# Output projection of a two-layer decoder trunk as seven block products, with its weights prepared during stick attention

## The chip, the cores and the metric

The kernel runs on one core of a Trainium2 chip. The metric is the device time of one execution in microseconds (us), as a median of several runs. PE is TensorE (matmuls), DVE is VectorE, ACT is ScalarE, POOL is GpSimd, SP is the engine whose queue issues nearly all DMAs.

## What is computed

Two layers of a decoder on 1024 tokens with 1024 features, in float32. Each layer adds two mixers and a gated ConvFFN to the residual x:

```
for l in range(2):
    h = rmsnorm(x, norm1[l]);  proj = h @ w_in[l]          # q, k, v of two mixers, and gates
    o_a = dilated_mixture(...)                             # windows of 128, 512 and 2048 tokens, 4 heads each
    o_b = stick_breaking_attention(...)                    # 4 heads, swept in blocks of 128 queries
    g_a, g_b = split(sigmoid(gate_pre + b_gate[l]))
    merged = g_a * (o_a @ w_br[l, :256]) + g_b * (o_b @ w_br[l, 256:])
    x = x + merged @ w_o[l]                                # the output projection
    h2 = rmsnorm(x, norm2[l])
    a, v = split(h2 @ w_up[l])
    x = x + (gelu(causal_conv(a)) * v) @ w_down[l]
return rmsnorm(x, norm_f)
```

## The kernel before

**Numbers in two parts.** PE multiplies fp32r operands, which hold fewer bits than float32. Each operand is therefore two tiles, a rounded high part and the low rest. `split` (L143) makes them: a cast on ACT (L146), a subtraction on DVE (L154). A product is three matmuls, hi x hi, hi x lo and lo x hi.

**Layout.** x lies with features on the 128 partitions: 8 chunks `e` of features, and two halves `n` of 512 tokens (`X[n]`, `xc(n, e)`). It is kept in DRAM (`xs`) during the mixers and fetched by `x_in` in pieces of 1 MB. `H[n]` holds the operand of the next product in two parts.

**Order.** PE's order is the order of the program text (`manual_schedule` over the whole kernel). On the other engines and on SP's queue a scheduler orders the ready instructions by their place in the text; `high_priority` moves one forward, manual dependencies move one back (`yields`, L1044, puts a DVE instruction behind the attention's latest one). Every engine then runs its queue in that order. In the FFN from the end of its second block to its last, ACT, DVE and POOL follow the text too (L1900). Tiles of one tag share a fixed number of buffers: "ot" and "bias" have one, "ql" and "wr" two, "wh", "wl", "xa" and "p4" four, "pt" and "e8" six; each of the four PSUM tags "ps", "s", "t", "o" has two banks.

**A layer.** `mixer` runs the input products of 18 pairs of 128 columns (`pair`, L1159), each as seven block products (Strassen's scheme in Winograd's form: sums of blocks take the place of the eighth product), while `attend` (L375) runs the attention items between their matmuls: 16 stick-breaking items, 4 near items, 16 far items. `Dense.share` (L309) counts the steps: one is half a block product, 6 matmuls, so a pair has 14. `pair_v` (L1289) transposes its values through a PSUM bank "o" (`v_t`) and splits them into a tile `vv` in buffer "ot" (L1295 to L1306); the attention's output `sb_o` uses bank "o" too.

**Branches.** For 16 pairs (n, e) the two branch products are multiplied by their gates (L1476) and added into `mrg` (L1481); `merged` (L1439) makes the two parts for the projection, the high one on ACT, the low one on POOL. `branch_in` (L1429) loads and splits the branch weights of two chunks. `X_AT` names the places where the four pieces of x are asked for.

**Output projection.** `wo_chunk` (L1323) is one of 16 units (n, e), all of half 0 first: load 128 columns of `w_o` (`weights`, L160), split them, 8 k x 3 matmuls, add the result to x on DVE (L1328), and add x squared into the norm's sum (`norm_add`: square on ACT L482, sum on DVE L484). `w_o` is so read and split twice, once for each half.

```
drive(first_half(), relay(*wo, primed=True), 2.5, 36)
```

After 36 steps (9 units) this line starts `first_half` beside the rest: `norm` for half 0 (PE totals L539, root on ACT, a scaling L556, a cast L558 and a subtraction L559 for each chunk) and `first_sum` (L529 and a split, four times). The norm of half 1 is handed to `ffn` and runs there beside the first FFN blocks (`up_plain` 0 and 1, then `up(2)` with seven products; `u_c` is one of its banks). `sums` and the later splits of the FFN run there on ACT and DVE.

**Seven products elsewhere.** `down` already computes the FFN's second half in this way: `into` tells which block of x each product's bank is added to, and one bank serves several products in a row.

Of the kernel before, what the change touches and what calls it, by code (L numbers as in the profile page):

```python
# [49 lines left out]
LEAD_N = 7  # L50
LEAD_T = 3
AHEAD_B = 3
X_AT = (3, 5, 14, 15)
AHEAD = 200
JOIN = 4
SEND = 4
# [4 lines left out]
def f32(ap):  # L61
    return ap.bitcast(F32)
# [3 lines left out]
def trunk_kernel(ctx, tc, x, norm1, w_in, b_gate, w_br, w_o, norm2, w_up, conv_w, conv_b, w_down, norm_f, out, depth=None, probe=None):  # L66
# [51 lines left out]
    xs = [dr.tile([P, KD, HF], F32, name=f"xs{n}") for n in range(2)]  # L118
    gs = dr.tile([KD, 2, P, 2, HF], F32, name="gs")
    gd = dr.tile([NF // 2, 7, P, 2, HF], F32, name="gd")  # L120
    obd = dr.tile([P, 2, T], F32, name="obd")
    tk = [dr.tile([2, 64, 4, 2, 4, 256], F32, name=f"tk{i}") for i in range(2)]
    tv = [dr.tile([2, 4, P, 2, 256], F32, name=f"tv{i}") for i in range(2)]
# [19 lines left out]
    def split(hi, lo, src, turn=None, behind=None):  # L143


        one = act.copy(hi, src)  # L146
        if behind:
            tc.add_manual_dep(one.ins, behind[0], NO_SYNC, reason="behind")
        if turn == "is":
            LAST["act"] = one.ins.name  # L150
        elif turn == "waits" and "act" in LAST:
            tc.add_manual_dep(one.ins, LAST["act"], NO_SYNC, reason="in turn")
        LAST["hi"] = one.ins.name
        two = dve.tensor_tensor(lo, src, f32(hi), ALU.subtract)  # L154
        if behind:
            tc.add_manual_dep(two.ins, behind[1], NO_SYNC, reason="behind")
        if turn == "is":
            LAST["dve"] = two.ins.name
        return two


    def weights(src, cols, place=None, eng=None):

        per = 512 // cols
        got = []
        src = src.rearrange("(k p) n -> p k n", p=P)
        for r in range(0, KD, per):
            raw = sb.tile([P, per, cols], F32, tag="wr", bufs=NRAW, name="w_raw")
            nc.sync.dma_start(raw, src[:, r : r + per, :])
# [12 lines left out]

    def product(o, pairs, first=True, last=True, share=False):

        n = len(pairs)
        quantum = 2 * 512 // o.shape[-1]
        for i, ((lh, ll), (rh, rl)) in enumerate(pairs):
            pe.matmul(o, lh, rh, start=(first and i == 0), stop=False, skip_group_check=share)  # L188
            pe.matmul(o, lh, rl, start=False, stop=False, skip_group_check=share)
            pe.matmul(o, ll, rh, start=False, stop=(last and i == n - 1), skip_group_check=share)  # L190
            if i % quantum == quantum - 1 and i < n - 1:
                yield
# [35 lines left out]
    class Dense:  # L228
# [4 lines left out]
        def __init__(self):  # L233
            self.main, self.plain, self.seven, self.done = [], [], [], set()
            self.side, self.later, self.hooks = [], {}, []
            self.now = self.nxt = None
            self.due, self.count = 0.0, 0
            self.started = False
            self.scored = self.applied = self.kq = self.v = 0
            self.rows, self.near, self.free = 0, 0, [0] * 4  # L240
            self.b = self.n = self.bv = 0

        def choose(self):
            if self.main and self.main[0][1] <= self.done and not (self.plain and self.main[0][3]):
# [64 lines left out]
        def share(self):  # L309
            self.count += 1  # L310
            for f in self.later.pop(self.count, ()):
                f()
            self.fetch()
            return True

# [131 lines left out]
    def h_part(n, k):  # L447
        return H[n][0][:, k, :], H[n][1][:, k, :]
# [9 lines left out]
    def xc(n, e, sub=slice(0, HF)):  # L458
        return X[n][e // 4][:, e % 4, sub]
# [13 lines left out]

    ACC = [None, None]

    def norm_add(n, e, first=False):

        if first:
            ACC[n] = sb.tile([P, HF], F32, tag="ql", bufs=2, name="nrm")
        acc = ACC[n]  # L480
        sq = acc if first else small("sq")
        act.activation(sq, xc(n, e), AF.Square)  # L482
        if not first:
            dve.tensor_tensor(acc, acc, sq, ALU.add)  # L484
# [559 lines left out]
    def yields(one):  # L1044

        for k in ("red", "dve"):
            if k in LAST:
                tc.add_manual_dep(one.ins, LAST[k], NO_SYNC, reason="in turn")
# [271 lines left out]
        return pair(dense, l, (OFF_G + e * P, OFF_G + D + e * P), False, put)  # L1320


    def wo_chunk(l, n, e):  # L1323
        w = weights(w_o[l][:, e * P : (e + 1) * P], P)
        yield
        o = bank("ps", "o_ps")
        yield from product(o, [(w[k], h_part(n, k)) for k in range(KD)])
        dve.tensor_tensor(xc(n, e), xc(n, e), o, ALU.add)  # L1328
        norm_add(n, e, e == 0)
        yield  # L1330

    def mixer(l, pending):
        R.clear()
# [7 lines left out]
            *((None, set(), f, True) for f in (pair_v(dense, l, 2), pair_kq(dense, l, 1, 1), pair_kq(dense, l, 2, 1))),  # L1341
        ]
        dense.side, dense.begin = block_sums(dense, l)
        dense.done |= {"K0", "K1", "V0", "V1", "V2", "V3"} | ({"wv"} if l else set())
        if l:
            next(vectors)
# [38 lines left out]
                items.append((f"T{pr}{i}", [f"F{8 * pr + i}"], [], RATE_T, lambda pr=pr, i=i, share=share: far_item(dense, pr, i // 4, i % 4, share)))  # L1385
        dense.fetch()
        attend(dense, items)
        oh = {}

        def branches():  # L1390
# [38 lines left out]
        def branch_in(i):  # L1429
            if i < len(todo):  # L1430
                e, wb = todo[i][1], big("br_w", F32R)
                raw = sb.tile([P, 4, 256], F32, tag="wr", bufs=NRAW, name="br_raw")
                nc.sync.dma_start(raw, w_br[l].rearrange("(k p) n -> p k n", p=P)[:, :, e * P : (e + 2) * P])
                parts_ = [[wb[:, h, 512 * q : 512 * q + 512].rearrange("p (k n) -> p k n", k=2) for h in range(2)] for q in range(2)]
                for q in (1, 0):
                    split(*parts_[q], raw[:, 2 * q : 2 * q + 2, :])
                wbs.append(parts_)

        def merged(n, e, m):  # L1439
            act.copy(H[n][0][:, e, :], m)  # L1440
            pool.tensor_tensor(H[n][1][:, e, :], m, f32(H[n][0][:, e, :]), ALU.subtract)

        wo = [wo_chunk(l, n, e) for n in range(2) for e in range(KD)]

        for i in range(3):
            gate_load(i)
# [11 lines left out]
        for i, ab in order:  # L1458
            n, e = todo[i]
            sl = slice(n * HF, (n + 1) * HF)  # L1460
            if i not in seen:
                if e == 0:
                    new_h(n)
                if i % 4 == 0:
                    wb = wbs.pop(0)
                if i in X_AT:
                    late_x = X_AT.index(i)
                    x_in(late_x // 2, late_x % 2)
            gt = gts[i]
# [10 lines left out]
            m = small("mrg")  # L1480
# [748 lines left out]
```

## Time and profile before

| | |
|---|---|
| median of 3 runs | 2602.6 us (2602.13 to 2603.34) |
| the profiled execution | 2603.86 us |
| its span, first to last instruction | 2602.2 us |
| granted TensorE clock | 1.000 |
| matmuls | 12647 |
| DMA | 470.60 MB, mean 181 GB/s |

The profile gives for each engine its busy time; for groups of equal instructions the line, the engine, the operation, output and inputs, the count, the sum and the mean duration; for a wait the instruction that ended it. Matmuls overlap: one of 389 ns starts 227 ns after another. A page's number behind "x" is a count.

### The profile page before, as it was taken

How to read it: one execution, taken by the hardware profiler on the slowest of the kernel's cores; microseconds unless marked ns; L12 is line 12 of the kernel's file. 1: busy time of each engine (PE TensorE's matmuls, PEld its weight loads, DVE VectorE, ACT ScalarE, POOL GpSimd, SP SyncE). 2: the span in 40 equal slices, each digit the busy share in tenths (PEclk: the TensorE clock that was granted, in tenths of full speed). 3: DMA queues.
4: the chain of work that ended last, by engine and by line, in shares of the span. 5: the costliest groups of instructions: out<-in, count | busy, mean ns of one | idle time of the engine just before them, and what ended most of it. 6: DMA issues, size and time to landing. Idle time of an engine off the chain costs nothing.

```text
span 2602.2 us, 36060 instructions
## 1 busy us (share of the span) xinstructions
PE 2589.6 (100%) x12647; PEld 2165.4 (83%) x12647; DVE 2084.7 (80%) x3485; ACT 1349.5 (52%) x2521; POOL 105.6 (4%) x145
## 2 busy tenths in 40 slices
PE   9999999999999999999999999999999999999999
PEld 8888888888888888888888888888888888888887
DVE  8877777796888888897677788777869888889965
ACT  6555666664554545422445555666645555554225
POOL 3000000030000000000000000000300000000000
PEclk9999999999999999999999999999999999999999
DMA  7434578863244454688344436798633354447863
GB/s 257 152 119 134 163 207 226 236 235 101 88 148 157 138 176 134 243 325 311 146 147 146 128 127 194 194 235 238 198 99 121 122 171 136 154 162 264 342 242 118
DMA packets 401409, 470.60 MB, mean 181 GB/s; under 512 B 24500, under 2 KB 315980, under 8 KB 399436
## 3 DMA queue, kind: packets, MB, share of 16 engines
q1 hardware_dynamic: 400364, 465.90, 55.2%
q0 software_dynamic: 704, 2.13, 0.4%
q8 instruction: 100, 1.64, 0.3%
q14 instruction: 81, 0.66, 0.1%
q10 hardware_dynamic: 160, 0.27, 0.0%
HBM read 305.59 MB, written 162.63 MB: 180 GB/s over the span
## 4 chain that ended last, share of the span: by engine, by line
PE 93%; DVE 3%; ACT 2%; DMA 1%; issue 1%; SPq 0%; POOL 0%; DVEq 0%; ACTq 0%
PE u_a L1060 6%; PE u_a L1061 6%; PE u_a L1059 6%; PE d_ps L1823 5%; PE d_ps L1825 5%; PE d_ps L1824 5%; PE i_a L1059 5%; PE i_a L1060 5%; PE i_a L1061 5%; PE u_c L1059 3%; PE u_c L1060 3%; PE u_c L1061 3%; PE i_c L1059 2%; PE i_c L1061 2%; PE i_c L1060 2%; PE o_ps L188 2%
## 5 line engine op out<-in xcount | busy, mean ns | idle before, releaser
L146 ACT CAST w_hi<-up_a 128x512 fp32r<-128x512 f32 x280 | 174.0, 622 | 277.1 <-DVE up_a L1677 120.8
L154 DVE TENSOR_TENSOR w_lo<-up_a,w_hi 128x512 fp32r<-128x512 f32 x280 | 189.3, 688 | 83.6 <-ACT w_hi L146 83.6
L146 ACT CAST w_hi<-in_a 128x512 fp32r<-128x512 f32 x252 | 156.2, 622 | 161.8 <-PE i_c L1060 35.6
L154 DVE TENSOR_TENSOR w_lo<-in_a,w_hi 128x512 fp32r<-128x512 f32 x252 | 172.7, 687 | 73.3 <-ACT w_hi L146 64.7
L1834 DVE TENSOR_TENSOR x<-x,d_ps 128x512 f32<-128x512 f32 x220 | 149.9, 683 | 60.3 <-PE d_ps L1825 57.0
L1059 PE MATMUL u_a<-hh,w_hi 128*128 128x512 f32 x320 | 124.5, 389 | 0.0
L1060 PE MATMUL u_a<-hl,w_hi 128*128 128x512 f32 x320 | 124.5, 389 | 0.0
L1061 PE MATMUL u_a<-hh,w_lo 128*128 128x512 f32 x320 | 124.5, 389 | 0.0
L1059 PE MATMUL u_a<-t_hi,w_hi 128*128 128x512 f32 x320 | 124.5, 389 | 0.0
L1060 PE MATMUL u_a<-t_lo,w_hi 128*128 128x512 f32 x320 | 124.5, 389 | 0.0
L1061 PE MATMUL u_a<-t_hi,w_lo 128*128 128x512 f32 x320 | 124.5, 389 | 0.0
L1823 PE MATMUL d_ps<-gd_in,w_hi 128*128 128x512 f32 x316 | 123.2, 390 | 0.0
L1825 PE MATMUL d_ps<-gd_in,w_lo 128*128 128x512 f32 x316 | 123.0, 389 | 0.0
L1824 PE MATMUL d_ps<-gd_in,w_hi 128*128 128x512 f32 x316 | 122.9, 389 | 0.0
L1059 PE MATMUL i_a<-hh,w_hi 128*128 128x512 f32 x288 | 117.9, 410 | 0.0
L1059 PE MATMUL i_a<-t_hi,w_hi 128*128 128x512 f32 x288 | 116.5, 404 | 0.0
L1061 PE MATMUL i_a<-hh,w_lo 128*128 128x512 f32 x288 | 113.1, 393 | 0.0
L1061 PE MATMUL i_a<-t_hi,w_lo 128*128 128x512 f32 x288 | 113.1, 393 | 0.0
L1060 PE MATMUL i_a<-hl,w_hi 128*128 128x512 f32 x288 | 112.9, 392 | 0.0
L1060 PE MATMUL i_a<-t_lo,w_hi 128*128 128x512 f32 x288 | 112.9, 392 | 0.0
L1823 PE MATMUL d_ps<-gd_in,wd 128*128 128x512 f32 x284 | 111.0, 391 | 0.0
L1825 PE MATMUL d_ps<-gd_in,wd 128*128 128x512 f32 x284 | 110.5, 389 | 0.0
(405 smaller groups left out, 7738.7 us busy)
## 6 DMA issues: line engine op xcount, KB each, us to landing
gd<-g SPq DMA_DIRECT2D x154, 512.0 KB, 3.1
gd_in<-gd SPq DMA_DIRECT2D x154, 512.0 KB, 6.2
up_a<-in_w_up_dram SPq DMA_DIRECT2D x80, 512.0 KB, 5.5
in_a<-in_w_in_dram SPq DMA_DIRECT2D x72, 512.0 KB, 5.4
wd_raw<-in_w_down_dram SPq DMA_DIRECT2D x22, 1024.0 KB, 11.4
gin<-gs SPq DMA_DIRECT2D x32, 512.0 KB, 4.3
w_raw<-in_w_o_dram SPq DMA_DIRECT2D x64, 256.0 KB, 2.8
gs<-u SPq DMA_DIRECT2D x48, 256.0 KB, 2.5
```

The source lines that it names most:

```text
L146: one = act.copy(hi, src)
L154: two = dve.tensor_tensor(lo, src, f32(hi), ALU.subtract)
L188: pe.matmul(o, lh, rh, start=(first and i == 0), stop=False, skip_group_check=share)
L1059: pe.matmul(o, w[0][:, c], rh, start=(first and i == 0), stop=False, skip_group_check=True)
L1060: pe.matmul(o, w[0][:, c], rl, start=False, stop=False, skip_group_check=True)
L1061: pe.matmul(o, w[1][:, c], rh, start=False, stop=(last and i == 3), skip_group_check=True)
L1823: pe.matmul(o, wh[:, c], gh, start=(i == 0 and k in (0, 4, 5)), stop=False, skip_group_check=True)
L1824: pe.matmul(o, wh[:, c], gl, start=False, stop=False, skip_group_check=True)
L1825: pe.matmul(o, wl[:, c], gh, start=False, stop=(i == m - 1), skip_group_check=True)
L1834: dve.tensor_tensor(x, x, o, ALU.add)
```

## The change

The output projection becomes seven block products in `out_proj`, with four blocks of 128 rows to a product. Features of the merged branches are divided into even and odd chunks, tokens into the two halves, output features into two halves of 512. The sums of weight blocks that this scheme needs and their two parts don't depend on data: `prepare` makes them for each layer during stick attention, a step of it per counted step from the 15th on, and keeps them in DRAM (`wod`, 7 x 4 tiles of 512 KB). The parts of the branch weights are made and kept in the same way (`brd`); `branch_in` only loads them. The sums of the merged branches are made on DVE beside the branches (`merged`) and beside the first products (`beside`). The sums of squares of both halves lie in buffer "ot". `first_half` starts after 42 of 56 steps of `out_proj`, with its first four steps spread by hand.

```
-X_AT = (3, 5, 14, 15)
+PREP = 14
...
+    wod = dr.tile([7, 4, P, 2, 512], F32, name="wod")
+    brd = dr.tile([4, P, 2, T], F32, name="brd")
...
         def share(self):
...
+            if self.prep and self.count > PREP:
+                next(self.prep, None)
...
-    def wo_chunk(l, n, e):
-        w = weights(w_o[l][:, e * P : (e + 1) * P], P)
...
+    def prepare(l):
+        many = 0
+        def out(src, there):
+            nonlocal many
+            t = small("w_two", F32R) if many % 2 else sb.tile([P, 512], F32R, tag="bias", name="w_two")
+            many += 1
+            act.copy(t[:, 0:256], src)
+            yields(dve.tensor_tensor(t[:, 256:512], src, f32(t[:, 0:256]), ALU.subtract))
+            nc.sync.dma_start(there, f32(t).rearrange("p (h n) -> p h n", h=2))
...
+        for e2 in range(4):
+            blocks = load(w_br[l].rearrange("(k p) n -> p k n", p=P)[:, :, 256 * e2 : 256 * e2 + 256])
+            for _ in range(3):
+                yield
+            for k, x in enumerate(blocks):
+                out(x, brd[e2][:, :, 256 * k : 256 * k + 256])
+                yield
+        for i in range(4):
+            for c in range(2):
+                raw = sb.tile([P, 2, 2, 256], F32, tag="ot", name="w_one")
...
+                for k, x in ((0, a11), (3, a22), (4, a12)):
+                    out(x, wod[k, i][:, :, col])
+                    yield
+                for k, dst, x, y, op in (
+                    (2, a11, a11, a21, ALU.subtract),
+                    (5, a21, a21, a22, ALU.add),
+                    (1, a22, a22, a11, ALU.subtract),
+                    (6, a12, a12, a22, ALU.subtract),
+                ):
+                    into(dst, x, y, op)
+                    out(dst, wod[k, i][:, :, col])
+                    yield
+    def out_proj(keep):
+        order = (0, 4, 1, 2, 3, 5, 6)
+        into = ((0, 0), (1, 0), (1, 1), (0, 1), (0, 0), (1, 1), (1, 0))
...
+        acc = sb.tile([P, 2, HF], F32, tag="ot", name="nrm")
+        def load(at):
...
+                if at % 2 == 0:
+                    if i % 2 == 0:
+                        t = sb.tile([P, 2, 2, 512], F32R, tag="ql", bufs=2, name="wo_in")
+                    nc.sync.dma_start(f32(t[:, i % 2]), wod[k, i])
...
+                else:
+                    w = [sb.tile([P, 512], F32R, tag=tag, bufs=4, name="wo_in") for tag in ("wh", "wl")]
+                    for h in range(2):
+                        nc.sync.dma_start(f32(w[h]), wod[k, i][:, h, :])
...
+        def beside(k, e):
+            c11, c12, c21 = keep[0, 0], keep[1, 0], keep[0, 1]
+            if k == 0:
+                dve.tensor_tensor(c11[:, e, :], c12[:, e, :], c11[:, e, :], ALU.add)
...
+                split(*sums[1][e], c11[:, e, :])
+            elif k == 4:
+                dve.tensor_tensor(c21[:, e, :], c21[:, e, :], c11[:, e, :], ALU.subtract)
...
+                split(*sums[2][e], c12[:, e, :])
+                if e == 3:
+                    x_in(1, 0)
+            elif k == 1:
...
+                split(*sums[3][e], c21[:, e, :])
+                if e == 3:
+                    x_in(1, 1)
+                    x_in(0, 1)
+        load(0)
+        load(1)
         yield
...
+        for at, k in enumerate(order):
...
+            for e in range(4):
+                o, c = banks[k][e], slice(e * P, (e + 1) * P)
+                for i in range(4):
+                    (wh, wl), (gh, gl) = ws[k][i], part(k, i)
+                    pe.matmul(o, wh[:, c], gh, start=(i == 0 and k in (0, 4, 5)), stop=False, skip_group_check=True)
+                    pe.matmul(o, wh[:, c], gl, start=False, stop=False, skip_group_check=True)
+                    pe.matmul(o, wl[:, c], gh, start=False, stop=(i == 3), skip_group_check=True)
+                    if i == 1:
+                        yield
+                n, f = into[k]
+                x = xc(n, 4 * f + e)
+                with tc.high_priority(offset=AHEAD):
+                    dve.tensor_tensor(x, x, o, ALU.add)
+                beside(k, e)
+                if k > 2:
+                    norm_add(n, 4 * f + e, e == 0 and k in (4, 5), acc[:, n, :])
+                yield
+            load(at + 2)
...
         def branch_in(i):
...
-                raw = sb.tile([P, 4, 256], F32, tag="wr", bufs=NRAW, name="br_raw")
-                nc.sync.dma_start(raw, w_br[l].rearrange("(k p) n -> p k n", p=P)[:, :, e * P : (e + 2) * P])
+                nc.sync.dma_start(f32(wb), brd[e // 2])
...
-                for q in (1, 0):
-                    split(*parts_[q], raw[:, 2 * q : 2 * q + 2, :])
...
         def merged(n, e, m):
...
+            hi, lo = H[n][0][:, e, :], H[n][1][:, e, :]
+            if n and e % 2 == 0:
+                t = small("mrg")
+                dve.tensor_tensor(t, m, keep[0, 0][:, e // 2, :], ALU.subtract)
+                split(hi, lo, t)
+                return
+            act.copy(hi, m)
+            pool.tensor_tensor(lo, m, f32(hi), ALU.subtract)
+            if n:
+                other = keep[1, 0][:, e // 2, :]
+                dve.tensor_tensor(other, m, other, ALU.subtract)
...
-                if i in X_AT:
-                    late_x = X_AT.index(i)
-                    x_in(late_x // 2, late_x % 2)
+                if i == 6:
+                    x_in(0, 0)
...
-            if i == 12:
-                next(wo[0])
+            if i == 9:
+                wo = out_proj(keep)
+                next(wo)
...
-        drive(first_half(), relay(*wo, primed=True), 2.5, 36)
+        side = first_half()
+        for n in (42, 0, 0, 2, 1):
+            for _ in range(n):
+                next(wo)
+            next(side)
+        drive(side, wo, 1.0)
```

More of the change, by code (lines that the diff above doesn't have):

```diff
@@ L241, in __init__ @@
             self.b = self.n = self.bv = 0
+            self.prep = None
         def choose(self):
@@ L474, in trunk_kernel, with norm_add @@
     ACC = [None, None]
-    def norm_add(n, e, first=False):
+    def norm_add(n, e, first=False, room=None):
         if first:
-            ACC[n] = sb.tile([P, HF], F32, tag="ql", bufs=2, name="nrm")
+            ACC[n] = room if room is not None else sb.tile([P, HF], F32, tag="ql", bufs=2, name="nrm")
         acc = ACC[n]
@@ L1320, in pair_gate, with into, load @@
         return pair(dense, l, (OFF_G + e * P, OFF_G + D + e * P), False, put)
-    def wo_chunk(l, n, e):
-        w = weights(w_o[l][:, e * P : (e + 1) * P], P)
-        yield
[L1326 to L1330, printed above, removed]
+    def prepare(l):
[7 more added lines that the diff above has]
+            nc.sync.dma_start(there, f32(t).rearrange("p (h n) -> p h n", h=2))
+        def into(dst, a, b, op):
+            yields(dve.tensor_tensor(dst, a, b, op))
+        def load(src):
+            raw = sb.tile([P, 4, 256], F32, tag="ot", name="w_one")
+            nc.sync.dma_start(raw, src)
+            return [raw[:, i, :] for i in range(4)]
+        for e2 in range(4):
[8 more added lines that the diff above has]
+                raw = sb.tile([P, 2, 2, 256], F32, tag="ot", name="w_one")
+                for j in range(2):
+                    src = w_o[l][(2 * i + j) * P : (2 * i + j + 1) * P, :].rearrange("p (f n) -> p f n", f=2)
+                    nc.sync.dma_start(raw[:, j], src[:, :, 256 * c : 256 * c + 256])
+                a11, a21, a12, a22 = (raw[:, j, f, :] for j in range(2) for f in range(2))
+                for _ in range(3):
+                    yield
+                col = slice(256 * c, 256 * c + 256)
+                for k, x in ((0, a11), (3, a22), (4, a12)):
[10 more added lines that the diff above has]
+                    yield
@@ L1343, in mixer @@
         dense.side, dense.begin = block_sums(dense, l)
+        dense.prep = prepare(l)
         dense.done |= {"K0", "K1", "V0", "V1", "V2", "V3"} | ({"wv"} if l else set())
@@ L1387, in mixer @@
         attend(dense, items)
+        for _ in dense.prep:
+            pass
         oh = {}
@@ L1431, in branch_in, with merge @@
                 e, wb = todo[i][1], big("br_w", F32R)
-                raw = sb.tile([P, 4, 256], F32, tag="wr", bufs=NRAW, name="br_raw")
-                nc.sync.dma_start(raw, w_br[l].rearrange("(k p) n -> p k n", p=P)[:, :, e * P : (e + 2) * P])
+                nc.sync.dma_start(f32(wb), brd[e // 2])
                 parts_ = [[wb[:, h, 512 * q : 512 * q + 512].rearrange("p (k n) -> p k n", k=2) for h in range(2)] for q in range(2)]
-                for q in (1, 0):
-                    split(*parts_[q], raw[:, 2 * q : 2 * q + 2, :])
                 wbs.append(parts_)
-        def merged(n, e, m):
-            act.copy(H[n][0][:, e, :], m)
-            pool.tensor_tensor(H[n][1][:, e, :], m, f32(H[n][0][:, e, :]), ALU.subtract)
-        wo = [wo_chunk(l, n, e) for n in range(2) for e in range(KD)]
+        keep = {}
+        def merge(n, e):
+            if e < 2 and (n, e) != (1, 1):
+                keep[n, e] = quarter("m_part")
+            return small("mrg") if n and e % 2 else keep[n, e % 2][:, e // 2, :]
+        def merged(n, e, m):
+            hi, lo = H[n][0][:, e, :], H[n][1][:, e, :]
[3 more added lines that the diff above has]
+                split(hi, lo, t)
+                return
+            act.copy(hi, m)
[3 more added lines that the diff above has]
+                dve.tensor_tensor(other, m, other, ALU.subtract)
         for i in range(3):
@@ L1479, in mixer @@
                 continue
-            m = small("mrg")
+            m = merge(n, e)
             dve.tensor_tensor(m, gt[:, 0, :], gt[:, 1, :], ALU.add)
```

25 lines of the change are left out of this document (added).

## The prediction

> **What bounds the kernel now.** I read the page from the top: busy shares first, then the chain that ended last.
>
> ```profile
> PE 2589.6 (100%) x12647; PEld 2165.4 (83%) x12647; DVE 2084.7 (80%) x3485; ACT 1349.5 (52%) x2521; POOL 105.6 (4%) x145
> PE 93%; DVE 3%; ACT 2%; DMA 1%; issue 1%; SPq 0%; POOL 0%; DVEq 0%; ACTq 0%
> ```
>
> TensorE (PE) is busy over the whole span and holds 93% of the chain; DVE is second, with a fifth of the span idle. So a removed matmul is worth its full pitch, and an added DVE instruction is free only where DVE idles. Next I read the chain in time order inside the output projection, for the pitch, and a table by window, for where DVE idles. The columns of the table are window, length, then the busy time of PE, PEld, DVE, ACT and POOL, the clock, the DMA share and GB/s.
>
> ```profile
> 625.84 0.23 PE o_ps L190
> ...
> 628.56 0.23 PE o_ps L190
> 90.00:280.00 190.00, 189.73 (x968) 157.54 (x967) 148.60 (x235) 103.87 (x212) 12.44 (x24) 1.00 0.42 130
> 530.00:581.00 51.00, 51.00 (x231) 42.19 (x229) 48.27 (x64) 31.78 (x54) 19.47 (x14) 1.00 0.73 250
> 590.00:668.00 78.00, 78.00 (x352) 64.59 (x350) 50.49 (x79) 33.23 (x56) 0.00 (x0) 1.00 0.34 100
> 637.00:668.00 31.00, 31.00 (x138) 25.53 (x137) 26.59 (x42) 15.89 (x27) 0.00 (x0) 1.00 0.32 94
> 668.00:719.00 51.00, 51.00 (x231) 41.95 (x230) 48.40 (x86) 28.66 (x50) 0.00 (x0) 1.00 0.29 93
> 1954.00:2005.00 51.00, 50.78 (x229) 41.74 (x228) 48.36 (x85) 28.28 (x50) 0.00 (x0) 1.00 0.29 93
> ```
>
> From the first row of the chain to the last lie 12 matmuls: 2.72/12 = 0.227 us each. The windows are, for layer 0, most of stick attention (90 to 280), the branches (530 to 581), the output projection (590 to 668), its end, and the FFN's first 51 us (668 to 719; layer 1's are 1954 to 2005). DVE idles 41.4 us of the 190, 27.5 of the 78, but only 2.6 of the 51. That last stretch ends in the one place where the chain leaves PE for long in layer 1:
>
> ```profile
> 1999.16 0.60 DVE up_a L1683
> 1999.76 0.60 DVE g L154
> 2000.36 0.61 DVE up_a L1684
> ...
> 2004.52 0.49 ACT u L1696
> ...
> 2005.05 0.50 PE u_c L1059
> PE u_c L1059 <- ACT u L1696: 0.3, 1, 0.3
> ```
>
> DVE, then ACT behind it, release the matmul `u_c` of the third FFN block. The wait is 0.3 us: at this point DVE's queue is exactly as late as PE can bear. I take its slack there as zero.
>
> **Removed: matmuls.** Per layer the old projection issues 2 halves x 8 chunks x 8 k x 3 = 384 matmuls of 128x512, the new one 7 products x 4 chunks x 4 blocks x 3 = 336. That is 48 less, in two layers 96 x 0.227 = **21.8 us**. The loops fix the count; that it isn't saved is no rival. If nothing else moved, the time would be 2602.6 - 21.8 = 2580.8.
>
> **Added in stick attention.** `prepare` issues per layer 16 + 8x7 = 72 casts on ACT, 72 + 32 = 104 DVE instructions, and on SP 72 writes of 256 KB and 20 loads (6.3 MB). All are 256 wide; the nearest rows, and how DVE instructions of 512 follow each other:
>
> ```profile
> L751 DVE TENSOR_TENSOR beta<-beta,stay 128x512 f32<-128x512 f32 x32 | 21.5, 682 | 1.6
> L751 DVE TENSOR_TENSOR beta<-beta,stay 128x255 f32<-128x255 f32 x16 | 6.7, 419 | 1.0 <-DVE stay L744 0.5
> L724 ACT ACTIVATE beta<-z 128x256 f32<-128x256 f32 x16 | 6.2, 390 | 4.9 <-PE z L650 4.9
> 703.12 0.68 DVE L1659 TENSOR_TENSOR b_f<-b_f,b_f 128x512 f32<-128x512 f32 x1
> 703.72 0.68 DVE L154 TENSOR_TENSOR t_lo<-b_f,t_hi 128x512 fp32r<-128x512 f32 x1
> 704.33 0.68 DVE L1662 TENSOR_TENSOR b_f<-b_f,b_f 128x512 f32<-128x512 f32 x1
> 159.38 0.68 DVE L154 TENSOR_TENSOR sbl<-sb_t,sbh 128x512 fp32r<-128x512 f32 x1
> 163.14 0.40 PE L665 MATMUL sb_o<-sbl,kv 128*66 128x256 f32 x2
> gs<-u SPq DMA_DIRECT2D x48, 256.0 KB, 2.5
> L169 SPq DMA_DIRECT2D w_raw<-in_w_o_dram x5: 367/368/368, 639.7 to 650.6; - x5
> ```
>
> An instruction of 0.68 us lets the next start after 0.60, so 0.08 us overlap; 256 wide I put at 0.42 - 0.08 = 0.34, and 104 x 0.34 = 35 us. The 108 steps, at 14 steps per weight pair, fill about these 190 us. DVE would be busy 184 of 190 us: covered on average, but with no spare. The second cover is lead: `sbl` is written 3.1 us before its matmul (159.38 + 0.68 against 163.14). ACT gains 72 x 0.39 = 28 us on 103.9: no bound. DMA gains 18.9 + 6.3 MB in 190 us, 133 GB/s beside 130: share 0.42 to about 0.85. SP spends 92 x 0.37 = 34 us on the issues; behind them in its queue stand the loads of keys, values and weight pairs, which are asked for some steps ahead. A cast into a `w_two` buffer waits until that buffer's last write has landed (2.5 us for 256 KB), and the sigmoids and `sbh` casts stand behind it on ACT; every second one takes the single buffer "bias". Bounds per layer: below nothing is excluded, as these 104 instructions replace none in this window; above, 43 - 41 = 2 us of overflow plus about 3 us if each bad stretch also uses up the lead. I take 1.5, nearer the low end, because the added instructions are ordered behind the attention's.
>
> [...]
>
> **Moved into the branches.** The eight splits of branch weights leave (each a cast and a subtraction), and about five of projection weights; 12 DVE instructions come: for the second half's even chunks a subtraction and a low part that POOL did, and for its odd ones another difference. 12 against 13: nothing changes on 48.27 busy of 51. SP's queue there now loads 1 MB per branch weight (was 0.5), 4 MB of projection weights and 1 MB of x (was 4): about 17 MB in 51 us where 250 GB/s makes 12.8. Cover is the three chunks' lead. Cost 0 to 2, I take 0.
>
> **DMA of the projection.** Each product needs 2 MB of ready parts, loaded while the product between runs: 48 x 0.227 = 10.9 us.
>
> ```profile
> gd_in<-gd SPq DMA_DIRECT2D x154, 512.0 KB, 6.2
> x<-xs SPq DMA_DIRECT2D x8, 1024.0 KB, 6.1
> 540.00:550.00 10.00, 10.00 (x45) 8.29 (x45) 8.90 (x11) 4.67 (x9) 4.29 (x4) 1.00 0.90 340
> ```
>
> At 340 GB/s 2 MB last 6.2 us; with 1 MB of x ahead in the queue 9.3, plus issue and landing about 1.5. That just fits 10.9. If x comes late, its add holds the accumulating bank, and PE behind it. 0 to 4 per layer, I take 0.5.
>
> **The end of the projection, the main cost.** Before, half 0 of x was final after 8 of 16 chunks, 43.5 us before the end. Now its last block (the fifth product) leaves two products, 21.8 us; the norm's first scaling may start after 44 of 56 steps, 12 x 6 x 0.227 = 16.3 us before the end. The norm, `first_sum` and the x adds of the last two products then crowd DVE ahead of a stretch that has no room. Count from 637.0, where the old norm starts, to 719:
>
> ```profile
> L556 DVE SCALAR_TENSOR_TENSOR b_f<-x,g,nrm_b x8: 737/741/748, 637.0 to 653.1; 128x512 f32<-128x512 f32 x8
> L529 DVE TENSOR_TENSOR s<-b_f,b_f x4: 681/681/684, 661.4 to 669.2; 128x512 f32<-128x512 f32 x4
> L1328 DVE TENSOR_TENSOR x<-x,o_ps x6: 677/686/689, 638.4 to 665.6; 128x512 f32<-128x512 f32 x6
> L484 DVE TENSOR_TENSOR nrm<-nrm,sq x6: 681/682/693, 640.2 to 667.4; 128x512 f32<-128x512 f32 x6
> L154 DVE TENSOR_TENSOR w_lo<-w_raw,w_hi x11: 682/685/693, 639.0 to 666.2; 128x512 fp32r<-128x512 f32 x11
> ```
>
> DVE was busy 26.59 + 48.40 = 75.0 us. Out go the old projection's 6 adds, 6 sums of squares and 7 of the 11 low parts (4 are the FFN's): 19 x 0.60 = 11.4. In come 7 adds and 7 sums of squares after the norm may start: 8.4. That is 72.0 us of work in 16.3 + 51 = 67.3: **4.7 us too much per layer**, and before it DVE can do none of it, since x isn't final and the FFN weights' buffers are held by the sixth product. From below: `first_sum` (8 instructions, 4.8 us) isn't needed until the third FFN block's fifth product, so all could slide: 0. From above, with 3 us of gaps: 8. I take 5. It doesn't matter whether PE stands still at the FFN's first weights or at `u_c`: the queue is the same.
>
> **Sum.** 21.8 - 2 x (1.5 + 0 + 0.5 + 5) = 7.8 us. The profiled execution took 2603.86 (span 2602.2 and 1.7 around it), 1.3 over the median of 2602.6; the gain is a difference and applies to either: 2602.6 - 7.8 = **2594.8**. About 0.2% (5.2 us) is what a measurement of this kernel can tell from no change.
>
> **Rivals.** *Nothing stalls.* `first_sum` slides behind, the lead covers stick attention; only 1 us goes per layer: 2602.6 - 21.8 + 2 = 2583. For it: in the branches DVE is busy 48.27 of 51 us and PE all 51. Against: the 0.3 us wait at `u_c`.
>
> *The gain is eaten.* The end costs 8 and stick attention 2.5 per layer: 2602.6 - 21.8 + 21 = 2602. For it: the 2.6 idle of 51.
>
> *Slower: one buffer held.* The raw weights of `prepare` sit in the only buffer of tag "ot" for 7 to 10 steps, about 18 us, one after the other; `pair_v` needs the same buffer for `vv` four times in this window.
>
> ```profile
> 240.00 0.60 PE L1295 MATMUL v_t<-ident,u 128*128 128x128 f32 x4
> 240.35 0.42 PE L663 MATMUL sb_o<-sbh,kv 128*128 128x256 f32 x2
> 241.20 0.59 ACT L1300 CAST vv<-v_t 128x512 fp32r<-128x512 f32 x1 [1.24 <-DMA sv<-vv]
> ```
>
> ACT's copy already waits 1.24 us for that buffer. A later `vv` keeps `v_t` in one of two banks "o", which `sb_o` needs 0.35 us behind on in-order PE; each `vv` then waits for the one before to be stored (3 us) and converted (1.3). Once the raw weights hold the buffer past the second `v_t`, PE stops for 4.5 to 9 us per layer. At 7.5 with the rest of the sum: 2594.8 + 15 = 2610. Against: ready instructions may run ahead of their step.
>
> **How the numbers follow.** The forecast (faster by 5.2 to 15) 0.42, nothing stalls 0.17, eaten (within 5.2) 0.19, slower 0.22. Faster 0.59, same 0.19, slower 0.22. The range 2582 to 2613 leaves out a little on either side; the forecast's own is 2588 to 2597.4.
>
> **What would show it.** Right: 96 matmuls fewer; 76 us per layer for the seven products (336 x 0.227); DVE full from the rescaling of half 0 to the third FFN block, with PE waiting there some 5 us per layer, on FFN weights or `u_c`; PE waits in stick attention under 2 us per layer. Wrong: a PE wait on bank "o" or `vv` near the first `v_t`; waits on `wo_in` or x; or no waits at the end.

## The result, and the profile after

The changed kernel takes 2699.26 us (2697.25 to 2703.17, four runs) for 2602.97 of the kernel before (2602.13 to 2603.68): slower, with a ratio of 1.0372 (1.0354 to 1.0390). The forecast was 2594.8, and the range ended at 2613. The profiled execution took 2700.12 us, its span 2698.4; the mean granted clock was 0.984, where it had been 1.000.

The rows of the page that answer to those of before, matmuls and engines, then the granted clock in 40 slices:

```profile
PE 2602.4 (96%) x12551; PEld 2164.6 (80%) x12551; DVE 2150.6 (80%) x3701; ACT 1361.9 (50%) x2609; POOL 111.4 (4%) x137
...
PEclk9998999999999999999999989999999999999999
```

The 96 matmuls are gone: 12551 for 12647. Yet PE now idles 4% of the span, and it was busy longer than before, 2602.4 us for 2589.6: some matmuls ran slower. The list of PE's waits names who ended them (columns: us in total, times, the longest):

```profile
PE u_ps L192 <- DVE w_lo L156: 15.1, 2, 7.5
PE v_t L1300 <- DVE vv L1306: 13.2, 2, 6.7
PE v_t L1300 <- DVE ob L678: 9.7, 2, 5.1
PE br_ps L190 <- DMA br_w<-brd: 9.0, 3, 4.3
PE sb_o L668 <- DVE ob L678: 8.5, 2, 4.5
PE i_c L1064 <- ACT u L1217: 7.2, 4, 2.2
PE z L654 <- ACT stay L730: 6.7, 6, 2.7
PE sb_o L668 <- DVE vv L1306: 6.7, 2, 3.3
```

To place the loss I matched PE's matmuls of the two traces in order and followed how late each starts (the delay ledger). In layer 0 the delay grows to 43.6 us in stick attention (90 to 330 us), stays flat until the branches, grows there by 6.4, shrinks by 11.8 in the projection, and grows by 9.9 at the FFN's first matmuls: 48.1. Layer 1 repeats it: 41.8 + 7.5 - 10.9 + 9.8 = 48.2. Together 96.3, as measured. The table by window shows the same (columns as in the prediction; the fourth stretch is 78 us of the seven products):

```profile
90.00:280.00 190.00, 166.82 (x797) 135.07 (x797) 149.14 (x274) 98.68 (x223) 9.31 (x19) 0.94 0.66 211
240.00:260.00 20.00, 14.63 (x63) 11.73 (x63) 14.64 (x28) 7.25 (x17) 0.86 (x2) 0.83 0.58 178
260.00:280.00 20.00, 10.21 (x46) 8.05 (x45) 9.67 (x19) 6.88 (x14) 0.00 (x0) 0.74 0.43 152
...
626.00:704.00 78.00, 78.00 (x352) 64.63 (x350) 47.91 (x75) 21.95 (x38) 2.05 (x2) 1.00 0.47 176
```

Seven products run without a gap. In stick attention PE does 797 matmuls where it did 968, and in the worst 20 us no engine is full: PE 10.21, DVE 9.67, ACT 6.88, DMA 0.43. Nothing there lacks throughput; engines wait for each other. The timeline of ACT just before shows how (start, length, instruction, and in brackets the idle time before it and what ended it):

```profile
243.72 0.58 ACT L148 CAST sbh<-sb_t 128x512 fp32r<-128x512 f32 x1
...
247.78 0.41 ACT L1337 CAST w_two<-w_one 128x256 fp32r<-128x256 f32 x1 [2.71 <-DMA wod<-w_two]
248.09 0.62 ACT L148 CAST w_hi<-in_a 128x512 fp32r<-128x512 f32 x1
252.82 0.40 ACT L1337 CAST w_two<-w_one 128x256 fp32r<-128x256 f32 x1 [4.11 <-DMA w_one<-in_w_o_dram]
253.13 0.47 ACT L148 CAST sbh<-sb_t 128x384 fp32r<-128x384 f32 x1
253.63 0.37 ACT L677 COPY fold<-sb_o 64x256 f32<-64x256 f32 x1
...
267.55 0.59 ACT L1305 CAST vv<-v_t 128x512 fp32r<-128x512 f32 x1 [0.49 <-DVE w_two L1338]
271.92 0.59 ACT L1305 CAST vv<-v_t 128x512 fp32r<-128x512 f32 x1 [3.79 <-DMA sv<-vv]
```

A cast of `prepare` stands at the head of ACT's queue until a transfer lands: first the last write out of its buffer (2.71 us), then the load that it reads (4.11 us). The attention's `sbh` and `fold` come right behind the second cast, 0.3 and 0.8 us later. `fold` could have run since 248.1, when the matmuls of its `sb_o` ended (247.67 in PE's rows below); it ran at 253.63, DVE's `ob` behind it at 254.11, and only this freed the bank for PE's `v_t` at 254.57. The load was late itself: SP's queue held two writes before it, and "ot" the tile before it, and both waited for the low part that DVE made at 248.22 from the cast of 247.78:

```profile
245.79 3.40 SPq L1339 DMA_DIRECT2D wod<-w_two  x2
249.24 1.28 SPq L1361 DMA_DIRECT2D w_one<-in_w_o_dram  x2
```

The first `vv` waits for the buffer "ot" until the last raw weights in it are converted, 24 us after the first `v_t` (243.89) and 13 after the second, and the second `vv` until the first is stored. PE's side of it:

```profile
243.89 0.60 PE L1300 MATMUL v_t<-ident,u 128*128 128x128 f32 x4
...
247.67 0.40 PE L670 MATMUL sb_o<-sbl,kv 128*66 128x256 f32 x2
...
254.57 1.12 PE L1300 MATMUL v_t<-ident,u 128*128 128x128 f32 x4 [5.14 <-DVE ob L678]
...
268.92 1.11 PE L1300 MATMUL v_t<-ident,u 128*128 128x128 f32 x4 [6.44 <-DVE vv L1306]
...
273.38 0.66 PE L668 MATMUL sb_o<-sbh,kv 128*128 128x256 f32 x2 [3.35 <-DVE vv L1306]
```

### The profile page after: what moved, and what is told of

It reads as the page before. It is cut to its first block, busy times and chain, and to the rows that moved or that the text cites. A ratio compares the mean times of both kernels' runs of the same rounds, so it can differ in the third digit from the quotient of the medians.

```text
span 2698.4 us, 36486 instructions
## 1 busy us (share of the span) xinstructions
PE 2602.4 (96%) x12551; PEld 2164.6 (80%) x12551; DVE 2150.6 (80%) x3701; ACT 1361.9 (50%) x2609; POOL 111.4 (4%) x137
## 5 line engine op out<-in xcount | busy, mean ns | idle before, releaser
L1337 ACT CAST w_two<-w_one 128x256 fp32r<-128x256 f32 x144 | 57.5, 410 | 111.0 <-DVE w_one L1342 43.8
L1973 PE MATMUL d_ps<-gd_in,wd 128*128 128x512 f32 x284 | 111.0, 391 | 0.0
```

Of the source, the lines that this page charges most:

```text
L1337: act.copy(t[:, 0:256], src)
L1973: pe.matmul(o, wh[:, c], gh, start=(i == 0 and k in (0, 4, 5)), stop=False, skip_group_check=True)
```

## The experiments

The theory, "held queue": in stick attention `prepare` puts instructions that wait for transfers, buffers or other engines at the head of in-order queues, and holds the single buffer "ot" when `vv` needs it. Rivals: too many instructions for DVE; too much traffic; engines and transfers that slow each other down. The two smaller losses, at the branches and at the end, are tested apart.

**Which part of `prepare`: all left out, engines alone, transfers alone, a pause.** The first three let the projection load constants, as the expectations say.

```
# e1:  dense.prep = nothing;  wo_in and br_w load constants (woz, brz)
# e2:  out() without its write, sources = ones.to_broadcast([P, 256])
# e3:  loads and writes alone, the writes straight from w_one
# e4:  if self.prep and self.count > PREP and not 92 < self.count < 109:
```

> prepare is left out (the projection and the branches load constants of the same size from DRAM, written once). The ledger of the two traces puts some 43 us per layer on stick attention, 6 on the branches, 9 on the end of the projection, and 11 gained by it. If all that stick attention lost comes from prepare: 2699 - 86 = 2613 (2605 to 2620), with PE waits in the window from 90 to 330 us back under 1 us per layer and the waits at the branches and at the FFN's first weights still there. If the loss lies in the new projection's own order or buffers: above 2680.

> prepare keeps its 72 casts and 104 DVE instructions of 256 columns per layer at the same steps, but they read a constant: no loads, no writes, no buffer 'ot'. Theory 'held queue' (casts at the head of ACT's in-order queue wait for transfers, and the raw weights hold the buffer that vv needs): within 6 us of the kernel without prepare, so about 2613 to 2620. Rival 'too many instructions for DVE': most of the 86 us stay, 2670 to 2700.

> prepare keeps its 20 loads into 'ot' and its 72 writes of 256 KB per layer, written straight from the loaded tile, but no cast and no DVE instruction (so the writes carry unsplit data and the projection loads constants). Rival 'traffic' (25 MB more in these windows slow everything): 2680 to 2700. 'Held queue': nothing on ACT or DVE waits for a transfer but vv for its buffer, so between the kernel without prepare (2613) and 2640, with PE waits on v_t alone.

> prepare makes no step in the 16 counted steps from 93 to 108, in which pair_v of the first group turns its values through buffer 'ot'; all else is as in the changed kernel. If the shared buffer 'ot' (the rival of the prediction, one buffer held) is the main cause, the four waits on v_t and sb_o go, 38 us in both layers by the list of waits, and the half-speed stretches behind them: 2640 to 2660. If the casts that wait for landings are the main cause: 2690 or more.

Measured: 2619.16, 2627.87, 2629.32 and 2679.52 us (before: 2602.93). Without `prepare` 80 us go. Of the 2619 some 5 us are, as an estimate, the writing of the constants, which delays the start by a wait of 3.3 us that the changed kernel hasn't got, and slow matmuls after it (2.2 us beyond a wait of 7.55 in the last section); so 2614, as the ledger had it. The wait, and the window of stick attention, as full as before the change:

```profile
PE x_t L2213 <- ACT w_hi L2200: 3.3, 1, 3.3
```

```profile
90.00:280.00 190.00, 189.73 (x966) 157.37 (x966) 148.24 (x234) 104.11 (x211) 11.43 (x24) 1.00 0.42 133
```

All engine work without transfers costs 9 us in both layers (at most 6 were expected), all transfers without engine work 10; together they cost 80. So neither DVE's count nor the traffic is the cause. Nor do the two slow each other down: a cast of `prepare` took 405 ns (median) without transfers and 406 with them, a low part 412 and 419, and a write into `wod` landed after 2.9 us without the engines' work and 2.5 with it. The cost comes of one waiting for the other. In e3 the raw weights hold "ot" for the same counted steps, and yet PE doesn't wait on `v_t` at all, where such waits had been expected: without casts that come late, the shared buffer alone doesn't stop PE there. The pause gains 20 where 40 to 60 were expected: "ot" is a part, not the whole.

**Loads or writes.**

```
# e7:  -  nc.sync.dma_start(there, ...)           (out() without its write)
# e8:  -  raw = sb.tile(..., tag="ot", name="w_one"); its loads   (sources = ones)
```

> prepare with its loads, casts and DVE instructions, but without its 72 writes per layer (the projection and the branches load constants instead). Casts then wait for loads, never for a w_two buffer to be stored. Engines alone cost 9 and transfers alone 10 us over the kernel without prepare (2619). If the landings of loads are what holds the queues: 2655 to 2690. If those of the writes are: 2630 to 2640.

> prepare with its casts, DVE instructions and 72 writes per layer, but without its 20 loads and without buffer 'ot' (the sources are constants, the projection and the branches load constants). If the landings of writes hold the queues: 2655 to 2690. If those of the loads and the buffer 'ot' do: 2630 to 2640. If either alone is harmless and only the two in a row are not, both kernels stay under 2640.

Measured: 2685.12 and 2655.90. Each alone does harm, as if both branches of the expectation were true: with loads 66 us over no `prepare`, with writes 37 (all three kernels write the constants). In the run without loads ACT waits for buffers to be stored, in layer 0 from 90 to 340 us:

```profile
ACT w_two L1339 <- DMA wod<-w_two: 27.2, 19, 5.1
ACT w_two L1339 <- DMA brd<-w_two: 14.0, 7, 3.7
```

and PE waits 2.6 us on `v_t` in all, for 13.2 + 9.7 in the changed kernel. The loads are the larger part and bring the `v_t` waits with them.

**More lead, and "ot" kept clear.** e9 gives a load five steps instead of three before its first cast. e10 does so too, and starts no load that would still hold "ot" in the steps in which `pair_v` turns its values.

```
# e9 and e10:
-            for _ in range(3):            # both places
+            for _ in range(5):
-PREP = 14                                 # 6 in e9, 2 in e10
# e10:
+            while not all(not a - 12 < dense.count < b for a, b in ((93, 107), (135, 149))):
+                yield
+            t = small("w_two", F32R) if many % 2 or dense.count > 134 else ...
```

> The changed kernel with five steps instead of three between a load of raw weights and the first cast of it (and prepare begins 8 steps earlier, so that it ends as before). Loads of 3 to 6 us then have about 9 instead of 5 us. If ACT and DVE are held by the landing of loads: 2650 to 2680. If buffer 'ot', now held longer by each raw tile when vv needs it, is the larger part: 2699 or more.

> As the last, but no raw tile is loaded that would still be held in the steps in which pair_v turns its values, so 'ot' is free for vv (prepare begins at step 3, and after step 134 its parts go to the buffers 'pt' alone). If loads and 'ot' together are the cause, only the waits for the landings of writes stay, worth 28 us by the kernel without loads: 2640 to 2660. If the loss comes with the amount of work and traffic: 2680 or more.

Measured: 2708.58 and 2675.27. Lead alone makes it 9 us slower, but e9 is no clean test. Its twelve tiles take 24 steps more in all, and it begins only 8 earlier; so `prepare` ends 16 steps later, not as before (its last low part is made at 351.0 us instead of 329.6 in layer 0). Where `pair_v` first turns its values, layer 0 loses 17 us instead of 25.5. But now `prepare` holds "ot" when `pair_v` turns the next ones, where the changed kernel has no wait on `v_t`, and PE waits there for 5.7 us. PE's waits on `v_t` in e9, over both places and layers:

```profile
PE v_t L1300 <- DVE vv L1306: 21.6, 7, 6.1
```

In e10 no wait on `v_t` is left, and the time falls by 33 from e9 and by 24 from the changed kernel; 2675 is more than the 2640 to 2660 expected. `prepare` now runs on beside the near windows, and waits stand there instead (PE's waits in e10, its window from 280 to 420, and that of the kernel without `prepare`):

```profile
PE o L670 <- DVE p0l L156: 8.0, 6, 1.6
...
PE i_b L1064 <- DVE u L1228: 6.1, 5, 2.5
```

```profile
280.00:420.00 140.00, 129.35 (x669) 106.87 (x668) 111.52 (x236) 86.38 (x204) 5.28 (x8) 0.96 0.77 227
```

```profile
280.00:420.00 140.00, 140.00 (x772) 119.37 (x771) 110.35 (x232) 87.25 (x204) 4.06 (x6) 1.00 0.68 191
```

**Which queue holds the rest.** From e10: DVE's sums two steps ahead of their casts (e13); casts on GpSimd (e14); no writes (e15). From e12 (below): all of `prepare`'s transfers in GpSimd's queue (e17); each write a step later, with a third `w_two` buffer (e18).

```
# e13: into(*sums.pop(0)) in the steps of k = 3, 4, 2, 5 instead of 2, 5, 1, 6
# e14: -  act.copy(t[:, 0:256], src)    +  pool.tensor_copy(t[:, 0:256], src)
# e17: nc.sync.dma_start -> nc.gpsimd.dma_start in prepare
# e18: if held: nc.sync.dma_start(*held.pop());  held.append((there, t));  many % 3
```

> The kernel of 2675 (raw tiles clear of vv, five steps of lead) with each DVE sum of weight blocks issued two steps before the cast that reads it. If casts that wait for sums hold ACT and with it the attention (8 to 20 us of ACT waits per layer in the changed kernel): 2645 to 2665. If those waits are harmless, as the kernel without transfers (2628) suggests: within 4 of 2675.

> The kernel of 2675 with the 72 casts per layer on GpSimd, whose queue holds little else here than the masks of beta. If ACT's queue, held at the head by casts, is what stops the attention: 2630 to 2650. If DVE's queue (its subtractions wait for the same casts) does as much, or GpSimd slows DVE: 2670 or more.

> The kernel of 2675 without the 72 writes per layer (projection and branches load constants; this costs about 5 us at its start). If the remaining loss is the waits for landings of writes: 2630 to 2645. If it is the loads and the sums: 2660 or more.

> The kernel of 2659 (raw tiles clear of vv, lead 5, branch weights earlier, end reordered) with prepare's loads and writes issued from GpSimd's queue instead of SP's. If what is left of the writes' cost is SP's held queue: 2630 to 2645. If it is the buffers that wait for their landing, or GpSimd's queue now holds the masks of beta in the same way: 2655 or more.

> The kernel of 2659 with each write of prepare issued at its next part, one step (about 1.7 us) later, when the low part is mostly there, and with a third w_two buffer in rotation ('bias' every third time instead of every second). If SP's queue, held 32 us per layer by writes that wait for DVE, costs time: 2640 to 2650. If the landings that the buffers wait for cost as much as before, or nothing of it matters: within 4 of 2659. Not below 2638, since engines and transfers of prepare alone cost 9 and 10 us over 2619 and the end keeps some 3 us per layer.

Measured: 2673.86, 2691.63, 2651.92, 2710.37 and 2656.14 (2651.17 to 2657.48). With the sums ahead ACT no longer waits for them (0.2 us for 11.1, from 90 to 400 us), but it waits longer for writes into `wod` (13.2 for 5.6), and the time stays (e13). The writes still cost 23 us, or some 28 without the 5 us that the constants cost e15; its time lies between the two that were expected. Moving work to GpSimd, which is almost idle (4% of the span in the changed kernel), made things worse, by 16 over e10 (e14) and by 51 over e12 (e17), as the second branch of each expectation had it. The waits of GpSimd in e17, 90 to 360 us, point to why: its queue now stands for DVE's low parts. Behind them in that queue are the attention's masks of `beta`, which its output needs:

```profile
POOL wod L1343 <- DVE w_two L1342: 52.1, 21, 6.8
POOL brd L1343 <- DVE w_two L1342: 15.0, 7, 4.4
```

By these waits it is the same mechanism on another queue; no run separates it from the longer instructions there (for e14 a cast of 683 ns instead of 406, see the last section). e18 gains 3 us on e12's 2659; its interval doesn't separate that from nothing, so whether SP's held head costs anything stays open.

**The branches.** `br_w` is asked for one chunk earlier.

```
                 if i % 4 == 0:
                     wb = wbs.pop(0)
+                    branch_in(i + 4)
...
-            if i % 4 == 1:
-                branch_in(i + 3)
```

> The changed kernel, with the branch weights of the next four chunks asked for one chunk earlier in the text (as the first of four begins instead of after the second), ahead of two loads of gates in SP's queue. If the wait on br_w comes from its place in SP's in-order queue, behind gate loads that wait for DVE: 4.3 us and about 2 of half-speed matmuls per layer go, 2684 to 2692. If the transfers there are limited by bandwidth (17 MB in 51 us): within 4 us of 2699.

Measured: 2696.34, a gain of 3 where 7 to 15 were expected. The number falls on the expectation's other branch, bandwidth, but its reason doesn't hold: the wait on `br_w` is gone, and the delay ledger falls by 6.6 us there; 3 of them come back at the projection's first products, whose operand POOL now delivers too late:

```profile
PE o_ps L1448 <- POOL hl L1585: 1.7, 2, 1.4
```

**The end.** First the FFN's low parts ahead in the queue (e5), then `first_sum` out of the way as well (e11), then all three edits with e10 (e12).

```
# e5:  with tc.high_priority(offset=AHEAD): split(hi, lo, raw)      (first FFN block)
# e11: e5, and
-            yield from first_sum()
+            up_plain(0, ..., {0: first_sum(), 2: both})
```

> The changed kernel, with the casts and low parts of the first FFN block's weights moved ahead of the norm in ACT's and DVE's queues (high priority). If the wait at the FFN's first matmuls is a matter of order (the low parts stand behind the whole norm and first_sum, though their casts are done 20 us earlier), the two waits of 7.5 us and the half-speed matmuls behind them go: 2680 to 2686. If DVE simply has too much work there, as the prediction had it, the wait moves to the norm's own parts or to u_c and the time stays above 2692.

> The changed kernel with the first FFN block's low parts ahead (as in the earlier run in which the wait moved to the norm of half 1) and with first_sum, 8 DVE instructions and 4.8 us per layer, moved from between the projection and the FFN into the first FFN block. If DVE has about 5 us too much before the norm of half 1: that wait falls from 7.5 to about 3 us per layer and the time to 2685 to 2692. If it isn't the amount: within 3 of 2699 or above.

> The three edits together: raw tiles clear of vv with five steps of lead, branch weights asked for one chunk earlier, low parts ahead and first_sum in the FFN. If the three losses add up as the ledger has them: the second kernel of this call, less 3 for the branches, less 8 to 14 for the end, 2625 to 2645; nowhere below the kernel before (2602), since engines and transfers of prepare alone cost 9 and 10 us over 2619. If the edits only move waits: within 5 of the second kernel.

Measured: 2707.28, 2696.06 and 2659.29. In e5 the wait doesn't go; it moves to the norm of half 1, at full size:

```profile
PE nrm_t L545 <- DVE nrm L490: 14.7, 3, 7.5
```

With eight instructions (4.8 us per layer) moved out of the way as well, it shrinks to this (e11):

```profile
PE nrm_t L545 <- DVE nrm L490: 6.0, 3, 2.9
```

So DVE has too much to do there, and order alone doesn't help. The time falls only to 2696, 4 above the 2685 to 2692 expected: per layer 4.6 us of wait go and some come back as new ones. All edits together (e12) reach 2659, 16 better than e10, within the expected sum (3 + 8 to 14), though alone the same edits had given 3 (e6) and 3 (e11); 40 better than the change, 57 worse than before; the expected 2625 to 2645 had e10 too low.

**A last set of edits together.**

> Raw tiles clear of vv, lead 5, sums two steps ahead, casts on GpSimd, branch weights one chunk earlier, low parts ahead and first_sum in the FFN. If all losses add up and the edits take them away: 2605 to 2630. If GpSimd's queue or its share of DVE's time takes ACT's place: 2650 to 2670.

Measured: 2663.56, 4 us over e12; by e13 and e14 the casts on GpSimd are what costs, but no run shows it beside the other edits. No version here beats the kernel before. What costs e12 its last 40 us over the kernel without `prepare` (more, if the losses at the branches and at the end, which that kernel still has, are counted out) isn't settled beyond this: the writes are 23 to 28 of e10's excess, and the rest is spread over short waits.

## Why the prediction was wrong

**What failed.** The step "Added in stick attention": 1.5 us per layer, bounds up to 5. Measured: 43 in the delay ledger, and 40 per layer by leaving `prepare` out (42.6 without the 5 us at that kernel's start). I compared busy sums with idle time (DVE 35 us of work in 41 idle) and called the work covered. That comparison held for the work itself: casts and DVE instructions alone cost 4.4 us per layer, close to the upper bound. It said nothing of instructions that wait. I had named the mechanism, "a cast into a `w_two` buffer waits until that buffer's last write has landed, and the sigmoids and `sbh` casts stand behind it on ACT", and gave it no term of its own. The reason for the low end, that added instructions are ordered behind the attention's, is what the trace refutes: `sbh` at 253.13 came behind a cast that had waited 4.11 us.

**The rival "one buffer held"** had the right place and mechanism, `vv`, `v_t` and bank "o". Its price was 4.5 to 9 us per layer; the steps of the ledger at `v_t` and the `sb_o` behind it add up to 22 in layer 0, 25.5 with the slow matmuls after them. About half of the 22 is not the buffer alone: `v_t` at 254.57 and `sb_o` at 304.19 waited for `ob`, the first of them because `fold` was held on ACT. Keeping "ot" clear gave back 24 in both layers, since other waits took the place. "Ready instructions may run ahead of their step" spoke against it; in the trace they didn't.

**Branches**: predicted 0, measured 7 per layer, 4.3 of it one wait for `br_w`. "Cover is the three chunks' lead" failed because SP's queue is in order: the load was issued only after four gate loads had stood for DVE (columns as in the timeline above):

```profile
599.05 8.05 SPq L1548 DMA_DIRECT2D gin<-gs  x4
607.19 0.38 SPq L1565 DMA_DIRECT2D br_w<-brd  x1
```

**DMA of the projection**: 0.5 predicted; no wait on `wo_in` or x. Right, or slightly too much.

**The end**: 5 predicted, 9.9 measured, of which 7.7 is the step at the wait and 2.2 slow matmuls behind it. The sum of DVE's work, 72.0 us in 67.3, pointed at the place, and that order doesn't matter (e5) was right too. Too small was the assumption that DVE works without a gap before: it idled 2.36 us for PE in the middle.

```profile
687.06 0.69 DVE L1455 TENSOR_TENSOR x<-x,o_ps 128x512 f32<-128x512 f32 x1 [2.36 <-PE o_ps L1449]
```

**Matmuls**: 96 fewer, 11.8 and 10.9 us less in the ledger, 10.9 worked out.

**Missing from the sum**: what a wait costs beyond itself, in the last section.

## What to carry to other kernels

Before hiding work beside a busy stage, compare its waits, not its busy time: for each added instruction ask what it waits for, how long that takes to land, and whose instruction is next in the same in-order queue. Work that costs 9 us without its transfers and 10 without its engines cost 80 with both. By e17, a queue that is idle isn't free when something critical sits in it, and more lead undoes itself where it holds a single shared buffer into the steps that need it (e9).

## What the runs showed of the hardware

After some of its longer waits PE's matmuls run at half speed for a while. After the 7.55 us wait for the FFN's low parts:

```profile
711.81 0.80 PE L192 MATMUL u_ps<-hh,w_lo 128*128 128x512 f32 x1 [7.55 <-DVE w_lo L156]
712.40 0.63 PE L190 MATMUL u_ps<-hh,w_hi 128*128 128x512 f32 x1
...
715.81 0.63 PE L192 MATMUL u_ps<-hh,w_lo 128*128 128x512 f32 x1
...
717.58 0.39 PE L191 MATMUL u_ps<-hl,w_hi 128*128 128x512 f32 x1
717.81 0.39 PE L192 MATMUL u_ps<-hh,w_lo 128*128 128x512 f32 x1
```

From 712.40 to 715.81 eight steps take 3.41 us, 0.426 each; from 717.58 the next starts after 0.23. By the delay against the kernel before, this costs 2.2 us beyond the wait. A wait of 2.66 us was enough, and the slow stretch then began 1.4 us after PE had started again and lasted about 3.5:

```profile
217.07 0.50 PE L654 MATMUL z<-kv,slots 128*128 128x512 f32 x1 [2.66 <-ACT stay L730]
...
218.46 0.63 PE L1064 MATMUL i_a<-hh,w_hi 128*128 128x512 f32 x1
...
222.28 0.39 PE L1065 MATMUL i_a<-hl,w_hi 128*128 128x512 f32 x1
```

The record of the granted clock in this trace agrees: the share is 1.0 or 0.5, and all its changes lie a whole number of 3.41 us apart. After the wait of 7.55 us it was 0.5 until 716.69, 4.9 us after PE had started again; after the wait of 2.66 us it was 0.5 from 218.34 to 221.75. A stretch with idle time wasn't always followed by half clock: the first below, with PE busy for 1.23 of 3.41 us, was followed by one at half clock; the last, with 1.61, by one at full clock (columns as in the prediction). What decides it no run shows.

```profile
214.93:218.34 3.41, 1.23 (x4) 0.76 (x5) 2.71 (x6) 3.12 (x8) 0.29 (x1) 1.00 0.70 225
218.34:221.75 3.41, 3.41 (x9) 2.63 (x9) 3.41 (x6) 2.20 (x5) 0.29 (x1) 0.50 0.70 255
...
1546.12:1549.53 3.41, 1.61 (x8) 1.01 (x6) 2.03 (x6) 2.42 (x7) 0.09 (x1) 1.00 0.85 257
```

GpSimd is no spare ScalarE: its cast of 256 columns took 683 ns (the group in e14), for a median of 406 on ACT (the tile `w_two` in the changed kernel).

```profile
L1340 POOL CAST w_two<-w_one 128x256 fp32r<-128x256 f32 x54 | 36.5, 683 | 134.0 <-DMA w_one<-in_w_o_dram 32.2 <-DMA wod<-w_two 21.5 <-DMA w_one<-in_w_br_dram 16.9
```

```profile
L1337 ACT CAST w_two<-w_one x72: 399/406/467, 76.9 to 329.2; 128x256 fp32r<-128x256 f32 x72
```
